# Softmax attention in a two-layer encoder: P times V in one fp32 pass on two column tiles, in place of two fp32r passes over a split V

## The chip, the cores and the metric

The kernel runs on one NeuronCore of one Trainium2 chip. The metric is the device time of one execution in microseconds (us), the median of several runs.

## What is computed

The reference is an encoder of two layers over 16 learned meta tokens and 1024 frames (L = 1040) of width 1024. A layer has a gated linear attention (GLA) and a softmax attention with a forget-gate bias (FoX) side by side, one output projection, and a gated feed-forward part with a short convolution. All of it is float32. The part that the change touches is the softmax attention: 8 heads of 64 channels, queries against all earlier keys.

```python
def block(inp):
    q_b, c_b, start = inp
    logits = (jnp.einsum('bqhd,bkhd->bhqk', q_b, kf)
              + c_b[..., None] - c_k[:, :, None, :])
    q_pos = start + jnp.arange(Q_BLOCK)
    logits = jnp.where(key_pos[None, :] <= q_pos[:, None], logits, -jnp.inf)
    return jnp.einsum('bhqk,bkhd->bqhd', jax.nn.softmax(logits, axis=-1), vf)
```

The output of a head then goes through an RMS norm per head. That norm takes out any common factor of a query's row, so the kernel works with unnormalised weights P = exp(logits - max) and brings the sum of P in only with the norm's epsilon.

## The kernel before

**Precision.** Most products are made of fp32r matmuls: an operand x is split into hi (x cast to fp32r by ScalarE) and lo (x - hi, by VectorE or GpSimd; `split`, L332), and a product takes the terms hi·hi, lo·hi and hi·lo (`mm3`, L217, three matmuls). Small products (the GLA state, L505 and L522; the column sums of the norms, L321 and L1116) use fp32 operands as they are. The narrow projection (L383 and L387) alternates matmuls of 128 and of 64 weight columns.

**Stages of a layer.** GLA and the first projections of FoX; then the attention stage with FoX for four pairs of heads p; then the output projection and the feed-forward part, which hold most of the time. In the attention stage the projections of the next pair (`fox_products`) and the gate of GLA (`gr_products`) are cut into units, and `Work.run` puts some of them between the steps of the current pair, so that TensorE has something to do while scores and exponentials are made.

**FoX.** Positions are cut into 9 tiles of 116 (the first has 112). A step (`fox_scores`, L643) takes one query tile i and one head e of the pair: scores S in PSUM over up to three chunks of keys (two matmuls each, L658 and L659), bias and running minimum on VectorE (L661), and P = exp on ScalarE (L673). Two steps later `fox_transposes` (L680) turns P by TensorE (L694, L687) into a PSUM tile `tr`, from where `split` brings it to SBUF as PT: hi by ScalarE (L335) and lo by VectorE (L336), which reads `tr` and hi. PT holds hi and lo for four key tiles and for the two query tiles of a group side by side (232 columns). A step later `fox_av` (L698) forms P times V for the group (7, 8), (5, 6), (3, 4), (1, 2) or (0): for each key tile t the weights are the 64 columns of V's hi beside the 64 of V's lo (128 weight columns), and there are two matmuls, one over PT's hi and one over its lo (L720). So rows 0 to 63 of the PSUM tile `av` hold the part of V's hi, rows 64 to 127 that of V's lo. Where it can, a matmul runs over 256 columns instead of the 232 needed. The last key tile is only needed by query tile 8 and has tiles of its own, PT2 and Vm. `av` goes to SBUF as `avs` (L723, ScalarE). When both heads are done, `fox_fold` (L725) turns it by TensorE (L733, `fo`) and adds the two halves (L736 on ScalarE, L737 on VectorE); the norm and `fox_store` follow.

V itself comes from a projection; `natural` in `fox_products` turns it (L591) and splits it for each head into V[e] (hi and lo), by ScalarE and VectorE.

**What sets the order.** The steps are listed with due times: transposes at step n + 2, `av` at n + 3, the fold at n + 4, the store at n + 6, with units of `Work` between. The tile framework's scheduler then fixes each engine's order ahead of the run (in the feed-forward part TensorE's order is written out by hand); an engine executes its instructions in that order and waits on semaphores. PSUM in the attention stage: `mm` 2 buffers, `S` 3, `tr` 2, `av` 1. PT has one buffer per part. The long-lived operands (`qA`, `kA`, `kL`, V) live in equal SBUF slots; in the attention stage two more are lent (`s.lent`).

Of the kernel before, what the change touches and what calls it, by code (L numbers as in the profile page):

```python
# [10 lines left out]
F32 = mybir.dt.float32  # L11
F32R = mybir.dt.float32r
# [21 lines left out]
FT, NT, FIRST = 116, 9, 112  # L34
# [100 lines left out]
class Kern:  # L135
# [417 lines left out]
    def fox_products(self, lyr, p, work, sp, pp, nm, q, w=None):  # L553
        nc = self.nc
        s = self.slots
        xs = nm["x"]
        rs = lambda c0, n: nm["r"][:, c0:c0 + n]
        q["qA"] = qA = [s.get(F32R, f"qA{e}") for e in range(2)]
        q["kA"] = kA = [s.get(F32R, f"kA{e}") for e in range(2)]
        q["kL"] = kL = [s.get(F32R, f"kL{e}", first=s.lent) for e in range(2)]  # L560
        q["V"] = V = [s.get(F32R, f"V{e}", (128, 8, 2, 64)) for e in range(2)]
        q["Vm"] = Vm = self.vmp.tile([FT, 2, 2, 64], F32R, tag="Vm", name="Vm", bufs=2)
        lo, hi = slice(0, 64), slice(64, 128)

        def ev_q(ps, c0, n):
            cs = slice(c0, c0 + n)
            t = sp.tile([128, 400 if self.vt_bufs == 3 else 348], F32, tag="vt", name="qt", bufs=self.vt_bufs)[:, :n]
            nc.vector.scalar_tensor_tensor(out=t, in0=ps, scalar=-0.125, in1=rs(c0, n),
                                           op0=ALU.mult, op1=ALU.mult)
            for e, (own, oth) in enumerate(((lo, hi), (hi, lo))):  # L570
                nc.scalar.copy(qA[e][own, cs], t[own])
                nc.gpsimd.tensor_tensor(out=qA[e][oth, cs], in0=t[own], in1=qA[e][own, cs].bitcast(F32),
                                        op=ALU.subtract)

        def ev_k(ps, c0, n):
            cs = slice(c0, c0 + n)
            t = sp.tile([128, 400 if self.vt_bufs == 3 else 348], F32, tag="vt", name="kt", bufs=self.vt_bufs)[:, :n]
            nc.vector.tensor_tensor(out=t, in0=ps, in1=rs(c0, n), op=ALU.mult)
            nc.scalar.copy(kA[0][:, cs], t)
            nc.gpsimd.tensor_tensor(out=kL[0][:, cs], in0=t, in1=kA[0][:, cs].bitcast(F32), op=ALU.subtract)  # L580
            if c0 + n == T:
                for k in (kA, kL):
                    for to, x, own in ((k[1], hi, hi), (k[1], lo, hi), (k[0], hi, lo)):
                        nc.sync.dma_start(to[x, :T].bitcast(F32), k[0][own, :T].bitcast(F32))

        def natural(vt, c0, n):
            t0 = 3 * [c for c, _ in CH_FOX].index(c0)
            tr = pp.tile([128, 4, 128], F32, tag="tr", name="tr")
            for j in range(3):
                o = self.start_of(t0 + j) - c0  # L590
                nc.tensor.transpose(tr[:FT, j, :], vt[:, o:o + FT], self.ident[:])  # L591
            nt = min(3, NT - 1 - t0)
            for e in range(2):
                d = slice(64 * e, 64 * e + 64)
                self.split(V[e][:FT, t0:t0 + nt, 0, :], V[e][:FT, t0:t0 + nt, 1, :], tr[:FT, :nt, d])
                if nt < 3:
                    self.split(Vm[:, e, 0, :], Vm[:, e, 1, :], tr[:FT, 2, d])

        def ev_v(ps, c0, n):
            vt = sp.tile([128, 400 if self.vt_bufs == 3 else 348], F32, tag="vt", name="vt", bufs=self.vt_bufs)  # L600
            nc.vector.tensor_tensor(out=vt[:, :n], in0=ps, in1=rs(c0, n), op=ALU.mult)
            self.later.append(lambda: natural(vt, c0, n))
        for m, ev in ((M_FQ + p, ev_q), (M_FK + p, ev_k), (M_FV + p, ev_v)):
            self.add_tile(work, pp, self.wm[lyr, m], xs, CH_FOX, ev, w=w)
            w = None

    def fox_free(self, q):
        self.slots.put(*q["qA"], *q["kA"], *q["kL"], *q["V"])

    def gr_products(self, lyr, h, work, ap, pp, nm, dst=None):  # L610
        nc = self.nc
# [68 lines left out]
    def fox_transposes(self, i, ci, P, PT, qoff, pp):  # L680
        nc = self.nc
        rows = self.rows_of(i)
        id_ = self.ident[:rows, :rows]
        tr = pp.tile([128, 4, 128], F32, tag="S" if ci == 2 else "tr", name="tr")
        qs = slice(qoff, qoff + rows)
        if ci == 2:
            nc.tensor.transpose(tr[:FT, 0, :FT], P[:FT, :FT], id_)  # L687
            self.split(PT[2][:, 0, :], PT[2][:, 1, :], tr[:FT, 0, :FT])
            return
        nt = min(4 * ci + 4, i + 1) - 4 * ci  # L690
        for j in range(nt):
            t = 4 * ci + j
            o, w = self.start_of(t) - self.start_of(4 * ci), FT if i else FIRST
            nc.tensor.transpose(tr[:w, 3 - j, :rows], P[:rows, o:o + w], id_)  # L694
        at = slice(4 - nt, 4)
        self.split(PT[ci][:w, 0, at, qs], PT[ci][:w, 1, at, qs], tr[:w, at, :rows])

    def fox_av(self, e, tiles, q, PT, avs, pp, part):  # L698
        nc = self.nc
        if part == 0:  # L700
            PT["av"] = pp.tile([128, 256], F32, tag="av", name="av")
        av = PT["av"]
        last = tiles[-1]
        width = FT * (len(tiles) - 1) + self.rows_of(last)
        ts = list(range(4 * part, min(4 * part + 4, last + 1)))
        if part == 0 and last:
            ts[:2] = 1, 0
        for t in ts:
            a, b = 0 if t <= tiles[0] else FT, width
            for i in range(2):  # L710
                if t == NT - 1:
                    w, x = q["Vm"][:, e, :, :], PT[2][:, i, :]
                else:
                    r, p = self.rows_of(t), 3 - t % 4
                    w, x = q["V"][e][:r, t, :, :], PT[part][:r, i, p, a:width]
                    if a == 0 and p < 3:

                        b = 256
                        x = PT[part][:r, i].rearrange("p a b -> p (a b)")[:, 2 * FT * p:2 * FT * p + b]
                nc.tensor.matmul(av[:, a:b], w.rearrange("p a b -> p (a b)"), x,  # L720
                                 start=(t == ts[0] and part == 0 and i == 0), stop=(t == last and i == 1))
        if last < 4 * part + 4:
            nc.scalar.copy(avs[:, e, :width], av[:, :width])  # L723

    def fox_fold(self, tiles, avs, den, ap, pp):  # L725
        nc = self.nc
# [113 lines left out]
    def fox_schedule(self, lyr, at, n, p, e, ti, i, tiles, Ps, st, q, ap, pp, mix3):  # L840
        PT = st[e]

        def T_(ci, P):
            def f():
                if ti == len(tiles) - 1 and ci == 0:
                    for key in range(2):
                        PT[key] = ap.tile([FT, 2, 4, 2 * FT], F32R, tag=f"PT{key}", name=f"PT{key}", bufs=1)
                    if i == NT - 1:
                        PT[2] = ap.tile([FT, 2, FT], F32R, tag="PT2", name="PT2", bufs=1)
                self.fox_transposes(i, ci, P, PT, FT * ti, pp)  # L850
            return f
        for ci, P in enumerate(Ps):
            at(n + 2, f"T{ci}", T_(ci, P))
        if ti == len(tiles) - 1:
            PT["nch"] = len(Ps)
        if ti:
            return

        def av(ci):
            def f():  # L860
                if e == 0 and ci == 0:
                    one = len(tiles) == 1
                    st["avs"] = ap.tile([128, 2, FT if one else 2 * FT], F32, tag="av1" if one else "avs",
                                        name="avs", bufs=1)
                self.fox_av(e, tiles, q, PT, st["avs"], pp, ci)
            return f

        def fold():
            st["on"] = self.fox_fold(tiles, st["avs"], st["den"], ap, pp)

        def store():
            self.fox_store(lyr, p, tiles, st["on"], ap, pp, mix3() if p == 3 else None)
        for ci in range(PT["nch"]):
            at(n + 3, f"av{ci}", av(ci))
        if e == 1:
            at(n + 4, "fold", fold)
            at(n + 6, "store", store)

    def attention(self, lyr, nm, hsrc, chunks, feed):
        tc, nc, s = self.tc, self.nc, self.slots  # L880
        with tc.tile_pool(name=f"aps{lyr}", bufs=2, space=PSUM, reuse_waits="tile") as pp2, \
# [3 lines left out]
            qs = [{} for _ in range(4)]  # L885
# [48 lines left out]
            self.att, self.vt_bufs = True, 2  # L934
            with tc.tile_pool(name=f"att{lyr}", bufs=2, reuse_waits="tile") as ap, \
                    tc.tile_pool(name=f"lent{lyr}", bufs=1, reuse_waits="tile") as lp:
                s.lent = s.add(lp, 2, f"a{lyr}_")
                box = {}
                KORD = (4, 5, 0, 1, 2, 3, 6)

# [799 lines left out]
```

## Time and profile before

| | |
|---|---|
| median of 3 runs | 2537.77 us (2534.29 to 2539.26) |
| span of the profiled execution | 2534.7 us |
| time of the profiled execution outside its span | not recorded |
| TensorE, VectorE, ScalarE, GpSimd busy in the span | 2485.4, 1769.3, 1274.8, 391.7 us |
| `av` matmuls (L720) | 800 records, 194.3 to 505.4 us and 1449.4 to 1760.3 us |
| lo of PT on VectorE (L336) | 240 instructions, 123.0 us |
| hi of PT on ScalarE (L335) | 240 instructions |

How to read it: PE is the matmul side of TensorE and PEld its weight loads, which overlap; DVE is VectorE, ACT ScalarE, POOL GpSimd, SP the queue that issues most transfers. A matmul record lasts until its last result is out, while the next one has long begun, so busy times and means of PE hide what a matmul takes from the others; distances between starts show that. In a row of the timeline stand start, length, engine, line, operation, output<-inputs, weights (rows*columns), shape of the moving operand, type and count; neighbouring records of one kind are merged. In the table by stretches each engine has its busy time and, in brackets, its instructions. In the list of waits stand who waited for whom, the sum in us, how often, and the longest.

### The profile page before, as it was taken

To read this page: it belongs to the slowest core of one execution; us is meant where nothing else is said; L and a number is where in the kernel's file an instruction comes from. 1 tells how busy PE (TensorE), PEld (TensorE's weight loads), DVE (VectorE), ACT (ScalarE), POOL (GpSimd) and SP (SyncE) were. 2 spreads that over 40 slices of the span, in tenths; PEclk is the share of its full clock that TensorE was granted. 3 is DMA by queue.
4 is the path that set the end of the run, shared out by engine and by line. 5 is a ranking of instruction groups with operands and counts; after the bars stand their busy time and mean duration, and the time that the engine had idled before them with its cause. 6 is when DMAs were issued, how large, how long until landed. Compare 5 with 4: busy or idle time off the path is not lost.

```text
span 2534.7 us, 46974 instructions
## 1 busy us (share of the span) xinstructions
PE 2485.4 (98%) x18430; PEld 2383.9 (94%) x18430; DVE 1769.3 (70%) x3508; ACT 1274.8 (50%) x2731; POOL 391.7 (15%) x568
## 2 busy tenths in 40 slices
PE   8999999999999999999999999999999999999998
PEld 7999999999999999999998899999999999997786
DVE  7656776769877777853665666777797777777545
ACT  6346666636444445641343466665464444455312
POOL 3023333210000000100210333331100000001002
PEclk9999999999999999999999999999999999999999
DMA  3232134342322224864312222243423222257622
GB/s 126 64 95 62 51 95 130 119 129 84 118 76 81 82 78 131 201 160 116 102 54 76 74 77 72 67 144 109 147 83 102 76 79 86 76 161 188 182 76 72
DMA packets 117933, 259.75 MB, mean 102 GB/s; under 512 B 14816, under 2 KB 32480, under 8 KB 117712
## 3 DMA queue, kind: packets, MB, share of 16 engines
q1 hardware_dynamic: 93408, 181.74, 23.1%
q0 software_dynamic: 22432, 72.71, 10.4%
q8 instruction: 144, 2.36, 0.4%
q10 hardware_dynamic: 1872, 2.31, 0.3%
q14 instruction: 77, 0.63, 0.1%
HBM read 176.11 MB, written 67.81 MB: 96 GB/s over the span
## 4 chain that ended last, share of the span: by engine, by line
PE 81%; DVE 11%; ACT 4%; DMA 2%; issue 2%; POOL 0%; SPq 0%; DVEq 0%; ACTq 0%; POOLq 0%
PE up L223 10%; PE up L221 10%; PE up L222 10%; PE mm L221 7%; PE mm L223 7%; PE mm L222 7%; PE down L221 5%; PE down L222 5%; PE down L223 5%; PE av L720 3%; PE tr L694 2%; DVE S L661 1%; PE S L658 1%; DVE x L1081 1%; PE S L659 1%
## 5 line engine op out<-in xcount | busy, mean ns | idle before, releaser
L223 PE MATMUL up<-x,hi 128*128 128x260 f32 (+1 forms) x2464 | 697.9, 283 | 4.0 <-DVE x L1081 4.0
L221 PE MATMUL up<-x,hi 128*128 128x260 f32 (+1 forms) x2464 | 698.6, 284 | 2.6 <-ACT x L1080 2.4
L222 PE MATMUL up<-x,lo 128*128 128x260 f32 (+1 forms) x2464 | 697.2, 283 | 0.0
L223 PEld LDWEIGHTS up<-x,hi 128*128 128x128 f32 x2464 | 466.9, 189 | 6.0 <-DVE x L1081 6.0
L221 PEld LDWEIGHTS up<-x,hi 128*128 128x128 f32 x2464 | 465.8, 189 | 3.6 <-ACT x L1080 3.6
L222 PEld LDWEIGHTS up<-x,lo 128*128 128x128 f32 x2464 | 466.2, 189 | 0.1
L1057 DVE TENSOR_TENSOR lo<-raw,hi 128x512 fp32r<-128x512 f32 x364 | 247.9, 686 | 171.6 <-ACT hi L1056 171.6
L221 PE MATMUL mm<-xh,hi 128*128 128x348 f32 (+4 forms) x1056 | 364.3, 345 | 0.0
L223 PE MATMUL mm<-xl,hi 128*128 128x348 f32 (+4 forms) x1056 | 340.2, 322 | 0.0
L222 PE MATMUL mm<-xh,lo 128*128 128x348 f32 (+4 forms) x1056 | 339.5, 322 | 0.0
L1056 ACT CAST hi<-raw 128x512 fp32r<-128x512 f32 x364 | 224.8, 620 | 143.8 <-PE up L223 93.2
L221 PEld LDWEIGHTS mm<-xh,hi 128*128 128x128 f32 x1056 | 200.1, 189 | 5.9 <-issue 5.3
L222 PEld LDWEIGHTS mm<-xh,lo 128*128 128x128 f32 x1056 | 200.1, 189 | 0.4 <-issue 0.3
L223 PEld LDWEIGHTS mm<-xl,hi 128*128 128x128 f32 x1056 | 198.9, 188 | 0.4 <-issue 0.3
L188 ACT CAST hi<-raw 128x512 fp32r<-128x512 f32 (+2 forms) x168 | 97.4, 580 | 182.2 <-PE down L223 105.4
L222 PE MATMUL down<-ah,lo 128*128 128x260 f32 (+1 forms) x528 | 169.0, 320 | 0.1
L221 PE MATMUL down<-ah,hi 128*128 128x260 f32 (+1 forms) x528 | 168.6, 319 | 0.0
L223 PE MATMUL down<-al,hi 128*128 128x260 f32 (+1 forms) x528 | 168.4, 319 | 0.0
L673 ACT ACTIVATE P<-S,m 116x460 f32<-116x460 f32 (+2 forms) x224 | 125.0, 562 | 71.8 <-DVE m L661 68.1
L336 DVE TENSOR_TENSOR PT<-tr,PT 116x464 fp32r<-116x464 f32 (+3 forms) x240 | 123.0, 515 | 47.3 <-ACT PT L335 45.7
L1039 DVE TENSOR_TENSOR raw<-raw,raw 128x512 f32<-128x512 f32 x198 | 129.5, 684 | 18.1 <-DMA raw<-in_wd_dram 15.5
L1270 POOL DMA_DIRECT2D actd<-cv x44 | 23.6, 536 | 764.3 <-DVE cv L1269 743.3
(283 smaller groups left out, 5618.8 us busy)
## 6 DMA issues: line engine op xcount, KB each, us to landing
raw<-in_wm_dram SPq DMA_DIRECT2D x326, 256.0 KB, 2.7
raw<-in_wd_dram SPq DMA_DIRECT2D x64, 256.0 KB, 3.6
actd<-cv POOLq DMA_DIRECT2D x22, 520.0 KB, 3.1
actd<-cv POOLq DMA_DIRECT2D x22, 512.0 KB, 2.9
cb<-cd SPq DMA_DIRECT2D x16, 520.0 KB, 3.7
st<-actd SPq DMA_DIRECT2D x14, 520.0 KB, 4.8
st<-actd SPq DMA_DIRECT2D x14, 512.0 KB, 5.1
kA<-kA SPq DMA_DIRECT2D x24, 260.0 KB, 4.2
```

What stands on the lines that cost most here:

```text
L188: nc.scalar.copy(hi[:, :n, :], raw[:, :n, :])
L221: nc.tensor.matmul(ps, wh, xh[:, c0:c0 + n], start=first, stop=False, skip_group_check=more)
L222: nc.tensor.matmul(ps, wl, xh[:, c0:c0 + n], start=False, stop=False, skip_group_check=more)
L223: nc.tensor.matmul(ps, wh, xl[:, c0:c0 + n], start=False, stop=last, skip_group_check=more)
L336: nc.vector.tensor_tensor(out=lo, in0=src, in1=hi.bitcast(F32), op=ALU.subtract)
L658: nc.tensor.matmul(S[:rows, :n], q["qA"][e][:, qs], q["kA"][e][:, c0:k1], start=True, stop=False)
L673: nc.scalar.activation(P[:rows, :n], S[:rows, :n], AF.Exp, scale=-1.0, bias=m[:rows, nch - 1:nch], accum_out=(den if nch == 1 else d3[:row ...
L694: nc.tensor.transpose(tr[:w, 3 - j, :rows], P[:rows, o:o + w], id_)
L720: nc.tensor.matmul(av[:, a:b], w.rearrange("p a b -> p (a b)"), x, start=(t == ts[0] and part == 0 and i == 0), stop=(t == last and i == 1))
L1039: nc.vector.tensor_tensor(out=q[out][:, :nk, :], in0=q[a][:, :nk, :], in1=q[b][:, :nk, :], op=op)
L1056: nc.scalar.copy(hi[:, :nk, :], src[:, :nk, :])
L1057: nc.vector.tensor_tensor(out=lo[:, :nk, :], in0=src[:, :nk, :], in1=hi[:, :nk, :].bitcast(F32), op=ALU.subtract)
```

## The change

P and V are no longer split. PT is an fp32 tile that ScalarE copies out of `tr` alone; V and Vm hold both heads unsplit and are copied by ScalarE, one copy where two splits were. `fox_av` issues one fp32 matmul for each key tile with the 64 columns of V as weights. Even key tiles write rows 0 to 63 of `av` (columns 0 to 63 of the array), odd ones rows 64 to 127. The fold is as before: it now adds the even and the odd tiles. With half the data, PT has two buffers; V takes one slot in place of two, and one slot is lent instead of two. Group (0) has only one key tile, so the lower half of its `avs` is set to zero on GpSimd. The padding to 256 columns and the swap of key tiles 0 and 1 go.

```diff
-        q["V"] = V = [s.get(F32R, f"V{e}", (128, 8, 2, 64)) for e in range(2)]
-        q["Vm"] = Vm = self.vmp.tile([FT, 2, 2, 64], F32R, tag="Vm", name="Vm", bufs=2)
+        q["V"] = V = s.get(F32, "V", (128, 8, 2, 64))
+        q["Vm"] = Vm = self.vmp.tile([FT, 2, 64], F32, tag="Vm", name="Vm", bufs=2)
...
-            for e in range(2):
-                d = slice(64 * e, 64 * e + 64)
-                self.split(V[e][:FT, t0:t0 + nt, 0, :], V[e][:FT, t0:t0 + nt, 1, :], tr[:FT, :nt, d])
-                if nt < 3:
-                    self.split(Vm[:, e, 0, :], Vm[:, e, 1, :], tr[:FT, 2, d])
+            nc.scalar.copy(V[:FT, t0:t0 + nt].rearrange("p t e d -> p t (e d)"), tr[:FT, :nt, :])
+            if nt < 3:
+                nc.scalar.copy(Vm[:].rearrange("p e d -> p (e d)"), tr[:FT, 2, :])
...
-            self.split(PT[2][:, 0, :], PT[2][:, 1, :], tr[:FT, 0, :FT])
+            nc.scalar.copy(PT[2][:], tr[:FT, 0, :FT])
...
-        self.split(PT[ci][:w, 0, at, qs], PT[ci][:w, 1, at, qs], tr[:w, at, :rows])
+        nc.scalar.copy(PT[ci][:w, at, qs], tr[:w, at, :rows])
...
-        if part == 0 and last:
-            ts[:2] = 1, 0
-        for t in ts:
-            a, b = 0 if t <= tiles[0] else FT, width
-            for i in range(2):
-                if t == NT - 1:
-                    w, x = q["Vm"][:, e, :, :], PT[2][:, i, :]
-                else:
-                    r, p = self.rows_of(t), 3 - t % 4
-                    w, x = q["V"][e][:r, t, :, :], PT[part][:r, i, p, a:width]
-                    if a == 0 and p < 3:
-
-                        b = 256
-                        x = PT[part][:r, i].rearrange("p a b -> p (a b)")[:, 2 * FT * p:2 * FT * p + b]
-                nc.tensor.matmul(av[:, a:b], w.rearrange("p a b -> p (a b)"), x,
-                                 start=(t == ts[0] and part == 0 and i == 0), stop=(t == last and i == 1))
+        for i, t in enumerate(ts):
+            a = 0 if t <= tiles[0] else FT
+            r = self.rows_of(t)
+            x = PT[2][:] if t == NT - 1 else PT[part][:r, 3 - t % 4, a:width]
+            w = q["Vm"][:, e, :] if t == NT - 1 else q["V"][:r, t, e, :]
+            half = slice(64 * (t % 2), 64 * (t % 2) + 64)
+            nc.tensor.matmul(av[half, a:width], w, x, start=t < 2, stop=t >= last - 1)
         if last < 4 * part + 4:
-            nc.scalar.copy(avs[:, e, :width], av[:, :width])
+            rows = slice(0, 128 if last else 64)
+            nc.scalar.copy(avs[rows, e, :width], av[rows, :width])
...
-                        PT[key] = ap.tile([FT, 2, 4, 2 * FT], F32R, tag=f"PT{key}", name=f"PT{key}", bufs=1)
+                        PT[key] = ap.tile([FT, 4, 2 * FT], F32, tag=f"PT{key}", name=f"PT{key}", bufs=2)
                     if i == NT - 1:
-                        PT[2] = ap.tile([FT, 2, FT], F32R, tag="PT2", name="PT2", bufs=1)
+                        PT[2] = ap.tile([FT, FT], F32, tag="PT2", name="PT2", bufs=2)
...
+                    if one:
+                        self.nc.gpsimd.memset(st["avs"][64:128], 0.0)
...
-                s.lent = s.add(lp, 2, f"a{lyr}_")
+                s.lent = s.add(lp, 1, f"a{lyr}_")
```

More of the change, by code (lines that the diff above doesn't have):

```diff
@@ L607, in fox_free @@
     def fox_free(self, q):
-        self.slots.put(*q["qA"], *q["kA"], *q["kL"], *q["V"])
+        self.slots.put(*q["qA"], *q["kA"], *q["kL"], q["V"])
     def gr_products(self, lyr, h, work, ap, pp, nm, dst=None):
```

## The prediction, made before the changed kernel ran

> **What bounds the kernel now.** The page comes first: spans, engines, then the chain that ended last.
>
> ```profile
> span 2534.7 us, 46974 instructions
> ...
> PE 2485.4 (98%) x18430; PEld 2383.9 (94%) x18430; DVE 1769.3 (70%) x3508; ACT 1274.8 (50%) x2731; POOL 391.7 (15%) x568
> ...
> PE 81%; DVE 11%; ACT 4%; DMA 2%; issue 2%; POOL 0%; SPq 0%; DVEq 0%; ACTq 0%; POOLq 0%
> ...
> L336 DVE TENSOR_TENSOR PT<-tr,PT 116x464 fp32r<-116x464 f32 (+3 forms) x240 | 123.0, 515 | 47.3 <-ACT PT L335 45.7
> ```
>
> TensorE (PE) is busy 98% of the span and holds 81% of the chain. VectorE (DVE) has 30% to spare over the whole, but that is an average, so the second view is the two attention stages alone. The matmuls of `av` run from 194.3 to 505 us and from 1449 to 1760 us; I took windows a little wider than that.
>
> ```profile
> core 0: us, PE busy (x) PEld busy (x) DVE busy (x) ACT busy (x) POOL busy (x), PEclk, DMA share, GB/s
> 190.00:512.00 322.00, 316.05 (x2232) 304.70 (x2231) 230.50 (x731) 209.49 (x631) 106.55 (x160) 1.00 0.30 90
> 1445.00:1767.00 322.00, 316.08 (x2234) 304.69 (x2233) 230.65 (x735) 209.45 (x631) 106.84 (x160) 1.00 0.30 91
> ```
>
> Here too PE is the full engine: it is idle for 322.00 - 316.05 = 5.95 us in the first layer and 5.92 us in the second, at a granted clock of 1.00. DVE is busy 72%, ScalarE (ACT) 65%. The third view is what PE waited for, from the answers for these two windows (three rows of the first; the fourth is the second layer's row for `tr`, and the rows for S and `av` read the same there):
>
> ```profile
> PE tr L694 <- DVE PT L336: 1.5, 2, 1.2
> PE S L658 <- ACT P L673: 1.1, 2, 0.7
> PE av L720 <- DVE PT L336: 0.4, 1, 0.4
> ...
> PE tr L694 <- DVE PT L336: 1.7, 3, 1.2
> ```
>
> The DVE step that the change deletes delays PE by 1.5 + 0.4 + 1.7 + 0.4 = 4.0 us in all, although it is 123.0 us of work. So the question is what the change does to PE's own work, not how much DVE work goes.
>
> **What P times V costs on PE now.** The groups with their shapes kept apart, the first and the last of six:
>
> ```profile
> L720 PE MATMUL av<-PT,V 116*128 116x256 f32 x448 | 96.4, 290 | 0.7 <-ACT PT L335 0.7
> ...
> L720 PE MATMUL av<-PT,Vm 116*128 116x116 f32 x32 | 5.6, 257 | 0.0
> ```
>
> The six are 448 matmuls of 256 columns, 128 + 64 of 232, and 96 + 32 + 32 of 116 or 112: 800, two for each of 400 key tiles. The mean of 290 ns is no price: matmuls are pipelined, and what one takes from PE is the distance between starts. The timeline has it:
>
> ```profile
> 196.50 0.40 PE L720 MATMUL av<-PT,V 116*128 116x256 f32 x2
> 196.74 0.38 PE L658 MATMUL S<-kA,qA 128*116 128x460 f32 x1
> ```
>
> Two matmuls of 256 columns take 196.74 - 196.50 = 0.24 us, so 0.120 us each, or 0.47 ns a column. By columns, 232 cost 0.109 and 116 or 112 about 0.055. The sum: 448 x 0.120 + 192 x 0.109 + 160 x 0.055 = 53.8 + 20.9 + 8.8 = **83.5 us**.
>
> **What it costs after.** There are 400 matmuls in full fp32: 320 of 232 columns and 80 of 116 or 112. An fp32 matmul on fp32 operands stands in this trace as the column sum of the norm:
>
> ```profile
> 575.65 0.28 PE L223 MATMUL up<-x,hi 128*128 128x260 f32 x1
> 575.77 0.60 PE L1116 MATMUL ssq<-r,ones 128*128 128x260 f32 x2
> 576.21 1.04 PE L1116 MATMUL ssq<-sq,ones 128*128 128x260 f32 x4
> 577.09 0.60 PE L1116 MATMUL ssq<-r,ones 128*128 128x260 f32 x2
> ```
>
> The code issues one matmul where the trace has two records, and four records take 577.09 - 576.21 = 0.88 us: 0.440 us a matmul of 260 columns, 1.69 ns a column, 3.6 times the present kind. So 232 columns cost 0.392 and 116 cost 0.196 us. One after the other, the 400 take 320 x 0.392 + 80 x 0.196 = 125.4 + 15.7 = 141.1 us. But even key tiles use columns 0-63 of the array and odd ones 64-127. Do two such tiles run side by side? The nearest rows are the state updates, fp32 with quarters of the array (64 rows by 64 columns), and their first step (16 rows, two column tiles only):
>
> ```profile
> 86.68 0.28 PE L223 MATMUL mm<-xl,hi 128*128 128x256 f32 x1
> 86.80 0.28 PE L221 MATMUL mm<-xh,hi 128*128 128x256 f32 x1
> 87.00 0.89 PE L505 MATMUL u<-gv,kd 64*64 64x128 f32 x24
> 87.82 0.39 PE L222 MATMUL mm<-xh,lo 128*128 128x256 f32 x1
> 88.05 0.28 PE L223 MATMUL mm<-xl,hi 128*128 128x256 f32 x1
> 88.17 0.28 PE L221 MATMUL mm<-xh,hi 128*128 128x256 f32 x1
> ```
>
> 24 records of 128 columns one after the other would be 24 x 0.108 = 2.6 us; they take 0.82. (0.89 - 0.27)/23 = 27 ns a record is a quarter of 0.108: four tiles at once. For two column tiles on the same rows there is
>
> ```profile
> 75.81 0.43 PE L505 MATMUL u<-gvm,kd 16*64 16x128 f32 x4
> 76.17 0.45 PE L221 MATMUL mm<-xh,hi 128*128 128x400 f32 x1
> ```
>
> where four records are over in 0.36 us, switches included, against 0.43 in turn. So I take full overlap, but only for neighbours in PE's order, because a full-width matmul between them uses all columns. The order of the changed program, counted: the 400 stand in 252 unbroken runs. Single: 102 of full width, 60 of half (the scheduler puts scores, transposes and projection pieces between). Even with odd: 44 runs of two, 16 of four. Runs of three: 16 (even, odd, half-width even), 10 others of full width. Four more are an odd one and a half. In full steps of 0.392: 102 + 60/2 + 44 + 16 x 2 + 16 x 1.5 + 10 x 2 + 4 = 256, so 256 x 0.392 = **100.4 us**. Against 83.5 now that is **+16.9 us** on PE; wholly in turn it would be 141.1 - 83.5 = +57.6. Those are the two ends; I take the first, as the nearest rows show overlap.
>
> In the Trainium skill, "TensorE: Matmul & The Clock Gate", Part 3 (Measured speedup vs the span model), three column tiles gave 2.38 times, not 3. At that efficiency two would give 1.59 times, and the side-by-side steps would add about 10 us to my sum (an estimate by that page); the 27 ns above say the overlap here is full.
>
> **Switching the array.** From 86.80 to 88.05 is 1.25 us, and its work is 0.12 + 24 x 0.027 + 0.12 = 0.89: entering and leaving the 64-row tiles costs 0.36 us. Does a 128-row, 64-column tile cost this? Such a matmul alternates with full ones in the narrow projection:
>
> ```profile
> 1295.25 0.28 PE L387 MATMUL mm<-xl,both 128*64 128x256 f32 x1
> 1295.37 0.28 PE L383 MATMUL mm<-xh,both 128*128 128x256 f32 x1
> 1295.49 0.28 PE L387 MATMUL mm<-xl,both 128*64 128x256 f32 x1
> 1295.60 0.28 PE L383 MATMUL mm<-xh,both 128*128 128x256 f32 x1
> ```
>
> Starts stand 0.12 apart both ways, as between equal ones: nothing for the switch. I take zero; up to 15 ns an edge would not show in these digits, 252 x 2 x 0.015 = 7.6 us, and the other end is 0.36 a run. The Trainium skill, "TensorEngine Tiling (Array Packing)", Key Properties, says that changing the tiling mode drains TensorE. The trace agrees for tiles of fewer rows and not for this one, but its tile begins at column 0 and no row has one that begins at 64.
>
> **The rest of the change.** It removes 240 DVE subtractions for PT (123.0 us) and those for V. ACT still copies each PT tile, so that edit saves no ACT time; V and Vm are copied once for both heads, a few short copies fewer. PE then waits for ACT's copy alone, and the transposes' PSUM buffers come free one DVE step earlier. What that is worth is bounded by PE's idle time in the stages, 5.95 + 5.92 = 11.9 us, and by nothing. I take **-5**: the 4.0 us put down to the DVE step, and half of the 2.2 us in which scores wait for P, since DVE's minimum stands ahead of it. What comes late next is ACT: exponentials and PT copies share its queue, and at 65% it has cover. PT has two buffers in place of one at the same size, V takes one slot per pair instead of two while one lent slot goes, and the 8 memory sets of `avs` lie on GpSimd, 33% busy, a step or more ahead of the fold that reads them; were GpSimd late, the fold's transposes and what stands behind them on PE would wait for it. The fold reads even and odd halves where it read high and low ones: same work. No DMA is moved.
>
> **Sum.** +16.9 - 5 = +11.9 on the profiled execution's 2534.7, so a span of 2546.6. The three runs have a median of 2537.77, 3.1 above this span, for what lies around it and the scatter: **2549.7 us**, +0.47%.
>
> **Rivals.**
> - *The waits pay for it.* PE's order is fixed ahead; with DVE lighter every wait in the two stages may end. For: DVE's column is the one that shrinks. Against: only 4.0 us of PE's idle time names the deleted step. All 11.9 us gone gives +16.9 - 11.9 = +5.0, 2542.8, just within the 0.2% (5.1 us) that a measurement here can tell from no change. It decides from 11.8 us on. To be faster by that much takes 22 us, and so waits that hide inside PE's busy time, which no row shows.
> - *The column tiles don't run side by side* (the change doesn't do what it says). For: no row has two 128-row tiles at once. Against: the 27 ns. +57.6 - 5 = +52.6: 2590.
> - *The array drains at column tiles.* By the mechanism of the 64-row rows, 0.36 us for each of 252 runs adds 91: +103, 2641. If only tiles at column 64 do it, 136 of the runs hold one: +49, +61, 2599. Against it: the 0.12 us rows. The Trainium skill's rule from TensorEngine Tiling (Array Packing), named above, is this one.
>
> **How the numbers follow.** Forecast 0.70; waits pay 0.14 (0.10 within 0.2%, 0.04 beyond it); no overlap 0.08; drains 0.08. Slower is 0.70 + 0.08 + 0.08 = 0.86, same 0.10, faster 0.04. The forecast's own spread is from 2543 to 2562: no wait saved (+5) and unseen edges (+7.6) at the top, all idle time at the bottom. The range goes a little below it, to 2536, for the waits, and to 2563; the two rivals at the top (0.16) and the faster tail are left out.
>
> **What would show it.** The `av` group should have 800 records, 64 columns wide, with pairs of records starting within some 10 ns in runs of two and four. Single ones of 232 columns should hold the next start off by 0.39 us. A projection matmul after them should start without a further 0.1-0.2 us. PE busy should grow from 316 to some 324 us per layer in stages that last 328, DVE there should fall from 230 to under 170 (half of 123.0 goes), and no wait of PE may name DVE's PT. Outside the stages nothing should move. If the stages grow by 26 us each, the overlap failed; by 30 to 51, the array drains; if they do not grow, PE had more waiting in it than its rows show.

## The result and the profile after

The changed kernel takes **2603.16 us** (median of 5 runs, 2602.36 to 2606.09) against 2534.89 before (5 runs): ratio 1.0269, 95% interval 1.0258 to 1.0280. It is slower by 68 us where I forecast 12, and outside my range. The rival that the array drains at column tiles, to which I gave 0.08 in two versions (2599 and 2641), is what happened.

The page of the changed kernel, the same rows as before:

```profile
span 2601.1 us, 46671 instructions
...
PE 2559.7 (98%) x18430; PEld 2341.5 (90%) x18430; DVE 1671.7 (64%) x3204; ACT 1275.7 (49%) x2699; POOL 394.3 (15%) x576
...
PE 56%; issue 29%; DVE 9%; ACT 3%; DMA 2%; POOL 1%; SPq 0%; POOLq 0%; DVEq 0%; ACTq 0%
...
L710 PE MATMUL av<-PT,V 116*64 116x232 f32 (+3 forms) x768 | 148.1, 364 | 0.1
```

The span grew by 66.4 us, PE's busy time by 74.3, and PE is still at 98%: nothing here says "switching". (The chain's 29% of "issue" stands where the rows of the feed-forward part stood; the time of those groups is what it was.) From the first to the last `av` record the stages grew from 311.1 to 346.9 us and from 310.9 to 346.5, 71.4 in all. That is 5 us more than the span grew, because the first `av` record comes earlier in the new order: at 191.2 us in place of 194.3 in the first layer, and in the second 1.5 us earlier, counted from the end of the first stage. Behind the last `av` record both kernels take 774 us, so the change acts in these stages and at their start alone. The table of the two stages, with the same margins around them as before:

```profile
core 0: us, PE busy (x) PEld busy (x) DVE busy (x) ACT busy (x) POOL busy (x), PEclk, DMA share, GB/s
187.00:545.00 358.00, 357.33 (x2241) 287.87 (x2240) 184.34 (x591) 210.61 (x619) 107.02 (x162) 1.00 0.27 80
1476.00:1834.00 358.00, 357.25 (x2243) 287.87 (x2242) 184.96 (x592) 210.53 (x619) 107.09 (x163) 1.00 0.27 80
```

DVE fell from 230.5 to 184.3 us a stage, and PE's idle time from 5.95 to 0.67. What PE still waited for in the first stage is one row, and it names no PT:

```profile
PE fo L723 <- ACT P L671: 0.4, 2, 0.2
```

So the waits that the change was to end did end. The timeline of the first stage shows what came instead. Two stretches, the second of single key tiles:

```profile
194.36 0.36 PE L692 MATMUL tr<-ident,P 116*116 116x116 f32 x2
194.66 1.00 PE L710 MATMUL av<-PT,V 116*64 116x232 f32 x8
195.59 0.61 PE L692 MATMUL tr<-ident,P 116*116 116x116 f32 x4
...
200.09 0.47 PE L656 MATMUL S<-kA,qA 128*116 128x460 f32 x1
200.49 0.61 PE L710 MATMUL av<-PT,V 116*64 116x232 f32 x2
201.03 0.46 PE L657 MATMUL S<-kL,qA 128*116 128x460 f32 x1
201.42 0.61 PE L710 MATMUL av<-PT,V 116*64 116x232 f32 x4
201.96 0.31 PE L692 MATMUL tr<-ident,P 116*116 116x116 f32 x1
```

In the last run (201.42) two key tiles, four records, take as long as one does at 200.49: even and odd run side by side, fully. In the run of four, the records start in pairs 7 ns apart, a pair every 0.196 us, as forecast (half of 0.392). That part of the forecast held. But from 200.09 to 200.49 a score matmul of 460 columns holds PE for 0.40 us, and between 201.03 and 201.42 the next one for 0.39; in the kernel before such a matmul held it for 0.22:

```profile
196.74 0.38 PE L658 MATMUL S<-kA,qA 128*116 128x460 f32 x1
196.96 0.29 PE L720 MATMUL av<-PT,V 116*128 116x256 f32 x1
```

The `av` of 200.49 takes 0.54 instead of 0.39. Every entry and every exit costs.

I worked this out over all 252 runs, from the ends of the records before and after a run, less what the run and the matmul after it hold PE for: median 0.336 us, mean 0.324, **sum 81.7 us**. In the kernel before, the same measure over its 274 runs has a median of 0.012 and a sum of 16.2, most of it at the 100 runs that hold half-width matmuls (116 or 112 columns).

### The profile page after: what moved, and what is told of

It is laid out like the page before. It is cut to its first block, busy times and chain, and to the rows that moved or that the text cites. A ratio compares the mean times of both kernels' runs of the same rounds, so it can differ in the third digit from the quotient of the medians.

```text
span 2601.1 us, 46671 instructions
## 1 busy us (share of the span) xinstructions
PE 2559.7 (98%) x18430; PEld 2341.5 (90%) x18430; DVE 1671.7 (64%) x3204; ACT 1275.7 (49%) x2699; POOL 394.3 (15%) x576
## 4 chain that ended last, share of the span: by engine, by line
PE 56%; issue 29%; DVE 9%; ACT 3%; DMA 2%; POOL 1%; SPq 0%; POOLq 0%; DVEq 0%; ACTq 0%
PE mm L221 8%; PE mm L223 8%; PE mm L222 8%; PE av L710 5%; PE down L221 5%; PE down L222 5%; PE down L223 5%; PE tr L692 3%; PE S L656 2%; PE S L657 2%; DVE x L1073 1%; DVE cv L1230 1%; DVE lo L1049 1%; PE wo L221 1%; PE wo L223 1%
## 5 line engine op out<-in xcount | busy, mean ns | idle before, releaser
L659 DVE CUSTOM_DVE_ANT_0 S<-S,cb 116x460 f32<-116x460 f32 (+2 forms) x144 | 81.0, 563 | 138.2 <-PE S L657 137.3
L710 PE MATMUL av<-PT,V 116*64 116x232 f32 (+3 forms) x768 | 148.1, 364 | 0.1
```

The source lines that it names most:

```text
L659: nc.vector.tensor_tensor_reduce(out=S[:rows, :n], in0=S[:rows, :n], in1=cb[:rows, c0:k1], scale=1.0, scalar=(BIG if ci == 0 else m[:rows, ...
L710: nc.tensor.matmul(av[half, a:width], w, x, start=t < 2, stop=t >= last - 1)
```

## The experiments

Theory S: each unbroken run of 64-column matmuls costs some 0.32 us for switching the array, beside its work. R1: the work is in turn and there is no switching cost. R2: the new order makes PE wait. The trace of the changed kernel speaks for S, but it does not say why the narrow projection, on which I had relied, shows no such cost.

**Full width.** No column tiles, and again 252 runs:

```diff
-            w = q["Vm"][:, e, :] if t == NT - 1 else q["V"][:r, t, e, :]
-            half = slice(64 * (t % 2), 64 * (t % 2) + 64)
-            nc.tensor.matmul(av[half, a:width], w, x, start=t < 2, stop=t >= last - 1)
+            w = (q["Vm"][:] if t == NT - 1 else q["V"][:r, t]).rearrange("p a b -> p (a b)")
+            nc.tensor.matmul(av[:, a:width], w, x, start=t == 0, stop=t == last)
...
```

> The changed kernel with 128 weight columns (V of both heads) in place of 64, so no column tiles; it adds the other head's V to each head, which leaves the work of TensorE as 400 fp32 matmuls strictly in turn, in 252 runs as before. Theory S (switching: each unbroken run of 64-column fp32 matmuls costs about 0.32 us beside its work, and pairs do overlap): 400 in turn cost 141 us in place of 100, but the 252 x 0.32 = 82 us go, so about 40 us faster than the changed kernel, 2560 to 2590 depending on how many waits come back. Theory R1 (pairs don't overlap and nothing is lost at the edges): no change, 2603. Theory R2 (the new order makes TensorE wait): no change or slower, 2603 or more.

Measured: 2570.57 us, 1.0137 of before (1.0120 to 1.0154), 33 us faster than the changed kernel although 41 us more of work stand in turn. S holds; R1 and R2 asked for no gain.

**The same at columns 0 to 63 only.** All key tiles in the lower half of `av`, 64 weight columns, in the same order of runs as full width:

```diff
-            half = slice(64 * (t % 2), 64 * (t % 2) + 64)
-            nc.tensor.matmul(av[half, a:width], w, x, start=t < 2, stop=t >= last - 1)
+            nc.tensor.matmul(av[0:64, a:width], w, x, start=t == 0, stop=t == last)
...
-            rows = slice(0, 128 if last else 64)
+            rows = slice(0, 64)
...
-                    if one:
+                    if True:
                         self.nc.gpsimd.memset(st["avs"][64:128], 0.0)
```

> The changed kernel with all key tiles on columns 0 to 63, in fp32, same 252 runs: no overlap, 141 us of work in place of 100. If the edge cost belongs to any 64-column fp32 tile: 41 us slower than the changed kernel, 2635 to 2650. If only tiles at column 64 cost it: the 82 us go and 41 come, 2560.

Measured: 2645.98 us (ratio 1.0439, 1.0425 to 1.0454). Against full width, with the same 400 fp32 matmuls in 252 runs of the same lengths, the 64-column form is 75 us slower: 0.30 us a run. And column 0 pays too, so the narrower version of my rival (only tiles at column 64) falls, though its 2599 lay near the result. The timelines of the two at the same place, first 64 columns, then 128:

```profile
195.65 0.37 PE L657 MATMUL S<-kL,qA 128*116 128x460 f32 x1
195.95 0.60 PE L709 MATMUL av<-PT,V 116*64 116x232 f32 x2
196.49 0.61 PE L692 MATMUL tr<-ident,P 116*116 116x116 f32 x4
```

```profile
195.58 0.37 PE L657 MATMUL S<-kL,qA 128*116 128x460 f32 x1
195.79 0.56 PE L709 MATMUL av<-PT,V 116*128 116x232 f32 x2
196.19 0.56 PE L692 MATMUL tr<-ident,P 116*116 116x116 f32 x4
```

From the score to the transposes it is 0.84 us in the first and 0.61 in the second; the rest of the 0.3 follows in the transposes (0.61 instead of 0.56) and what stands behind them.

The weight loads (PEld) at the same places show what TensorE does in this time, again first 64 columns, then 128:

```profile
195.95 0.19 PEld L709 LDWEIGHTS av<-PT,V 116*64 116x64 f32 x2 [0.33 <-issue]
196.48 0.19 PEld L692 LDWEIGHTS tr<-ident,P 116*116 116x116 f32 x2 [0.34 <-issue]
```

```profile
195.59 0.40 PEld L709 LDWEIGHTS av<-PT,V 116*128 116x128 f32 x2
196.00 0.53 PEld L692 LDWEIGHTS tr<-ident,P 116*116 116x116 f32 x4
```

At full width the load of V starts 0.01 us after the score ahead of it does. At 64 columns it starts 0.30 us after it, 0.07 before the record of the score ends, and the load for the transposes again 0.07 us before the last `av` record ends. TensorE takes no weights for the other shape until the matmul ahead is all but done: it drains. The same 0.07 us (0.071 to 0.072 in nearly all) stands at both ends of the 252 runs of this kernel and of the changed one; at full width it is 0.2 us or more in nearly all. Ends of matmuls are modelled, so what counts is that it is always the same and not its size.

**The same in fp32r.** Type alone changes (P and V rounded, one pass):

```diff
-        q["V"] = V = s.get(F32, "V", (128, 8, 2, 64))
+        q["V"] = V = s.get(F32R, "V", (128, 8, 2, 64))
...
-                        PT[key] = ap.tile([FT, 4, 2 * FT], F32, tag=f"PT{key}", name=f"PT{key}", bufs=2)
+                        PT[key] = ap.tile([FT, 4, 2 * FT], F32R, tag=f"PT{key}", name=f"PT{key}", bufs=2)
```

(and so for Vm and PT2; columns 0 to 63 as above.)

> The changed kernel with P and V rounded to fp32r (one pass, lo of both left out) and all key tiles on columns 0 to 63, 64 weight columns, 252 runs. Work: 320 x 0.109 + 80 x 0.055 = 39 us in place of 83.5 before. If 64-column tiles switch only in fp32: no edges, so 44 us faster than before less or more by waits, 2475 to 2495. If any 64-column tile in this place switches: 252 x 0.32 = 82 us on top, 2560 to 2575.

Measured: 2497.30 us (0.9858, 0.9844 to 0.9871). There are no edges: the median over its 252 runs is 0.015 us, and the weight loads do not wait (0.15 us or more before the end of the matmul ahead in nearly all). The timeline shows a single one between a projection and two scores:

```profile
208.59 0.32 PE L223 MATMUL mm<-xl,hi 128*128 128x348 f32 x1
208.74 0.27 PE L709 MATMUL av<-PT,V 112*64 112x232 f32 x1
208.85 0.38 PE L656 MATMUL S<-kA,qA 128*116 128x460 f32 x1
209.07 0.27 PE L709 MATMUL av<-PT,V 116*64 116x232 f32 x1
```

The distances are 0.15, 0.11 and 0.22 us: each the price of its columns, nothing more. The time is 2 us over the range that I gave.

**The narrow projection in fp32**, in the kernel before:

```diff
-                    self.nc.tensor.matmul(ps[0:64, :n], w[0][k][:, 0:64], xl[:, c0:c0 + n], start=False, stop=False)
+                    self.nc.tensor.matmul(ps[0:64, :n], w[0][k][:, 0:64].bitcast(F32), xl[:, c0:c0 + n].bitcast(F32),
+                                          start=False, stop=False)
```

> The kernel before with the 48 matmuls of 64 columns of the narrow projection in fp32 in place of fp32r, alternating with full fp32r ones as before (42 unbroken runs). More work: 48 x 347 columns x (1.69 - 0.47) ns = 20 us. If 64-column tiles switch only in fp32 (S by type): each run 0.3 us more, 13 us, so 2568, and the start after such a matmul of 256 columns stands about 0.7 us off in place of 0.43. If the type has nothing to do with it: 2555, and starts 0.43 us apart with no further gap. In the first layer some of it may hide behind the wait for the input.

Measured: 2566.09 us (1.0125, 1.0109 to 1.0141), 30 us more for 48 matmuls. The row on which my prediction leaned, with the type changed:

```profile
1318.26 0.39 PE L383 MATMUL mm<-xh,both 128*128 128x256 f32 x1
1318.57 0.65 PE L387 MATMUL mm<-xl,both 128*64 128x256 f32 x2
1319.15 0.39 PE L383 MATMUL mm<-xh,both 128*128 128x256 f32 x1
```

From one full matmul to the next it is 0.89 us; 0.12 and 0.43 are work, so 0.34 is switching. In fp32r the same pair took 0.23 (1295.37 to 1295.60). The weight loads start 0.07 us before the end of the matmul ahead at both ends of its 42 runs, and in fp32r mostly 0.3.

**bf16 on both column tiles** (the changed kernel with BF16 for V, Vm, PT and PT2 in place of F32, precision left out):

> The changed kernel with P and V rounded to bf16 (precision left out), on both column tiles, 240 runs. Work at one pass: 249 steps of some 0.10 us = 25 us. If the edge cost is fp32's alone: 50 to 60 us faster than before, 2465 to 2490. If tiles at column 64 switch whatever the type, those runs (about half) cost 0.3 us each: 2510 to 2530; if all runs do: 2545 to 2560.

Measured: 2517.22 us (0.9935, 0.9922 to 0.9949). The time falls into the band that I had given to "only column 64 switches", and the trace refutes that reading: over its 240 runs, single ones at column 0 cost 0.304 us (median of 110), those at column 64 also 0.304 (40), longer runs 0.26 to 0.30. All pay, and the weight loads have the same 0.07 us. The time is lower than 2545 because waits give way: beside the edges, the records of the two stages take some 9 us more than their kinds usually do here; in the kernel before it is some 19, and the 16 at its runs. It is 20 us slower than fp32r at one column tile, which has less overlap and no edges. A single one:

```profile
205.70 0.32 PE L223 MATMUL mm<-xl,hi 128*128 128x348 f32 x1
205.96 0.29 PE L710 MATMUL av<-PT,V 112*64 112x232 bf16 x1
206.17 0.46 PE L656 MATMUL S<-kA,qA 128*116 128x460 f32 x1
206.56 0.29 PE L710 MATMUL av<-PT,V 116*64 116x232 bf16 x1
```

The projection holds PE for 0.26 us in place of 0.16, the score for 0.39 in place of 0.21, and the bf16 matmul itself for 0.21 in place of 0.1.

**Without lo of P**, the kernel before with the DVE step left out, same matmuls:

```diff
-        self.split(PT[ci][:w, 0, at, qs], PT[ci][:w, 1, at, qs], tr[:w, at, :rows])
+        nc.scalar.copy(PT[ci][:w, 0, at, qs], tr[:w, at, :rows])
...
-                    w, x = q["V"][e][:r, t, :, :], PT[part][:r, i, p, a:width]
+                    w, x = q["V"][e][:r, t, :, :], PT[part][:r, 0, p, a:width]
```

(and so for the padded form and PT2.)

> The kernel before with VectorE's subtraction for PT left out and both fp32r matmuls reading hi, so TensorE's work is as before: it leaves out lo of P. It measures alone what the freed VectorE is worth. My prediction's term: 5 us, 2530. If the whole idle time of TensorE in the two stages hangs on it: 12 us, 2523. If the 27 us that the sum of work and switching has over the measured growth are relief from VectorE: 2508.

Measured: 2532.97 us (0.9987, 0.9978 to 0.9997): 2.7 us for 123 us of DVE records, nearer to the 5 of my prediction than to 12 or 27. DVE was not what this stage waited for.

**Fewer runs.** The changed kernel with its `av` matmuls at high priority:

```diff
-            nc.tensor.matmul(av[half, a:width], w, x, start=t < 2, stop=t >= last - 1)
+            with self.tc.high_priority(200):
+                nc.tensor.matmul(av[half, a:width], w, x, start=t < 2, stop=t >= last - 1)
```

> The changed kernel with its P times V matmuls at high priority, so that they stand in 108 unbroken runs in place of 252, with 200 full steps of 0.392 us in place of 256. Theory S: 144 x 0.32 = 46 us of switching and 56 x 0.392 = 22 us of lone steps go: 2535 if no wait comes back, up to 2555. Overlap without switching costs: 22 us go, 2581. R1 (in turn, no switching): no change, 2603. R2: no forecast, but waits of TensorE for P or PT should make up whatever stays.

Measured: 2566.73 us (1.0124, 1.0109 to 1.0139), 36 us faster than the changed kernel where S gave 48 to 68 and overlap alone 22. Fewer runs do cost less, but part comes back: a run that stands together early waits at its head for the copy of PT, which it did not before. PE's waits in this kernel:

```profile
PE av L711 <- ACT PT L694: 19.9, 32, 1.5
```

**Both heads in one run.** `fox_av` is called once for a group and issues both heads' key tiles alternately, the odd head on the opposite half:

```diff
+        with self.tc.high_priority(200):
+            ts = [*range(tiles[0], -1, -1), *tiles[1:]]
+            for t in ts:
+                for e in (1, 0):
...
+                    h = 64 * ((t + e) % 2)
+                    nc.tensor.matmul(av[h:h + 64, e, a:width], w, x, start=t == ts[0], stop=t == ts[-1], skip_group_check=True)
...
-        for ci in range(PT["nch"]):
-            at(n + 3, f"av{ci}", av(ci))
         if e == 1:
+            at(n + 3, "av0", av)
```

> The changed kernel with the P times V matmuls of both heads of a group in one unbroken run at high priority, odd head on the opposite column tile: 40 runs in place of 252, 180 steps of 0.392 us in place of 256. Theory S: 180 x 0.392 = 70.6 us of work and 40 x 0.32 = 13 us of switching, 83.4 in all, which equals the 83.5 us of the kernel before, so what the freed VectorE brings is left over: 2508 to 2530, faster than both kernels. If the switching cost were not per run: 256 - 180 = 76 steps, 30 us less than the changed kernel, 2573.

Measured: 2546.47 us (1.0046, 1.0032 to 1.0060): 57 us faster than the changed kernel, but above the 2508 to 2530 that I expected, and still not faster than the one before. Again the head of the run waits:

```profile
PE av L710 <- ACT PT L694: 19.6, 28, 1.4
```

**The same a step later**, with three PT buffers and four P buffers:

```diff
-P_BUFS = 5
+P_BUFS = 4
...
-            at(n + 3, "av0", av)
+            at(n + 4, "av0", av)
-            at(n + 4, "fold", fold)
-            at(n + 6, "store", store)
+            at(n + 5, "fold", fold)
+            at(n + 7, "store", store)
```

> The kernel of both heads in one run, with the run, the fold and the store one step later, three PT buffers and four P buffers in place of five: the same 40 runs and 180 steps. If the 20 us by which it lost were the waits of TensorE for ScalarE's copy of PT at the head of a run (9.8 us in the first layer's stage), they go: 2520 to 2535. If the waits only move, to scores that wait for P or to the fold, it stays at 2540 to 2550.

Measured: 2540.23 us (1.0022, 1.0012 to 1.0032), the case in which the waits only move. Those for PT shrink and others come:

```profile
PE fo L726 <- ACT P L671: 10.2, 10, 1.9
...
PE av L710 <- ACT PT L694: 6.0, 16, 0.7
```

The fold's transposes now wait behind exponentials on ACT. By price, 40 runs of column tiles (70.6 + 13 us) equal the two fp32r passes (83.5); I found no order in which the fp32 form wins.

**One pass over hi**, in the kernel before (V split, lo of P left out, one matmul for each key tile):

```diff
-            for i in range(2):
+            for i in range(1):
...
-                                 start=(t == ts[0] and part == 0 and i == 0), stop=(t == last and i == 1))
+                                 start=(t == ts[0] and part == 0 and i == 0), stop=(t == last))
```

> The kernel before with lo of P left out of the computation and only one fp32r matmul for each key tile, over hi, with 128 weight columns (V split as before). Half of the 83.5 us of P times V goes, nothing is tiled: 2533 - 42 + the waits that come back (in the one-pass run on 64 columns 37 of 44 us were kept), 2492 to 2503. If the price of the present matmuls were not the distance of their starts but something less, the gain is smaller.

Measured: 2490.27 us (0.9825, 0.9811 to 0.9839), 45 us for half of the 83.5 us, 2 us below the range that I gave. The price by distances of starts was right within some 3 us; the DVE step that is also left out is worth 2.7 alone, and half-width matmuls cost more than I took (below). It beats both kernels, but it gives up the low part of P, so it is a trade and no repair.

## Where the prediction was right and where it failed

- **What bounds the kernel:** right. PE's own work decides; 123 us of DVE work are worth 2.7 us.
- **Work of `av`, +16.9:** right in the main. The run of four above has its pairs 0.196 us apart, and half of the old work is worth 45 us (42 by my price). The old work was some 5 us dearer than 83.5: the last half-width matmul of a run holds PE for 0.112 us (median of 100) and not for my 0.055.
- **Overlap of the column tiles:** right, only for neighbours, and fully: a pair of records every 0.196 us, where one record alone takes 0.196. The Trainium skill, "TensorE: Matmul & The Clock Gate", Part 3 (Measured speedup vs the span model), has 2.38 times for three column tiles of 32 columns, which is short of three; two tiles of 64 columns in fp32 reach two here.
- **Switching the array, "I take zero":** wrong; this is the step that failed. I read zero off the narrow projection, which is fp32r. I put the switching cost of the state updates (0.36 us) down to their 64 rows, when they were also the nearest fp32 rows with fewer than 128 columns. Measured: 0.30 to 0.34 us a run in fp32 at column 0 (64 columns against full width, 75 us over 252 runs; the narrow projection turned to fp32), about as much in bf16, 0.015 in fp32r. The sign was in the trace before: at the state updates the weight loads wait to 0.07 us before the end of the matmul ahead, and at the narrow projection they don't. The Trainium skill's rule in "TensorEngine Tiling (Array Packing)", Key Properties, that a change of the tiling mode drains TensorE, agrees with the fp32 and bf16 rows; the fp32r rows show nothing of it.
- **Waits that go, -5:** too small. Work +16.9 and edges +81.7 make 98.6, the span grew by 66.4, so 32 us went elsewhere. About half of it is the 16.2 us at the runs of the kernel before, waits and the dearer half-width matmuls, which the 81.7 took the place of. Between the other records of the two stages, the time beyond what each kind usually takes from end to end fell from some 19 to some 8 us. The last 5 us are the earlier starts of the stages. So the kernel before had some 30 us of waiting (16.2 + 19, less the 5), and mostly not in PE's 11.9 us of idle time: a record of 0.28 us holds PE for 0.12, so a wait of up to some 0.16 us after it counts as busy. I had named such waits and set them aside because no row shows them. Freed DVE is little of it (2.7). The waits go because PE gets slower and the others keep up: the full-width kernel and the fp32r one at columns 0 to 63 have the same buffers and 252 runs each, differ by 102 us of work (141 and 39) and only by 73 us of time. Against the kernel before, 57.6 us of added work cost 35.
- **DVE, "under 170":** it came out as 184.3 us a stage. I subtracted the 123.0 us of the records, but records of DVE overlap: without these 240, its busy time in the kernel before would be 96 us less.
- **Rivals:** the drain had the right mechanism and the wrong price in the sum: 252 x 0.36 on top of everything gave 2641; an edge of 0.32 and the waits that gave way bring it to 2603. That its narrower version gave 2599 was luck. My two signs for it, a stage longer by 30 to 51 us and a next start held off by 0.1 to 0.2 us, came out as 35.7 us and, in the timeline above, as 0.18 us ahead of a run and 0.15 at its end.

What stays open: why a 64-column fp32r matmul at column 0 costs no switch. Nothing here separates a tile that fp32r does not use from a switch that it does not need; fp32r at column 64 was not tried. No run has bf16 at full width, so for bf16 the tile is not separated from the type; that its weight loads wait as the fp32 ones do speaks for the tile.

## What to carry to other kernels

A price for an operation must come from a row with the same operand type as well as the same shape: the same 64-column matmul switched the array in fp32 and bf16 and not in fp32r. Column tiles do overlap, but each unbroken run of them cost some 0.3 us here, so the runs must be long, and making them long has its own price in waits: even 40 runs in place of 252 did not win. Whether an operation drains the array can be read from the weight loads around it. In a busy TensorE short waits hide inside the records, so added work can cost much less than its own length (57.6 us cost 35) and freed helpers bring much less than theirs.

## What was not expected of the hardware

The switch of the array depends on the type: per run 0.33 us in fp32 (single key tiles of the changed kernel, 116 at column 0 and 46 at column 64 alike) and 0.30 in bf16, and 0.015 in fp32r, which was tried at column 0 alone. While it lasts, the next weight load stands still until 0.07 us before the end of the matmul ahead. An fp32 matmul of full width costs none (0.016 us a run in the full-width kernel). In none of these does PE look idle: its busy share in the stages of the changed kernel is 357.33 of 358 us.
